# Experts' weights in rows of 48 KB: eight groups of six units a pair in three large places, the last norm's tables in the first norm's place

## The chip, the cores and the metric

One core of a Trainium2 chip runs the whole layer in one launch. The metric is the device time of that launch in microseconds, as the median of several runs; less is better. All numbers below come from the runs of the kernel before the change and from one profiled execution of it.

## What is computed

One post-norm layer of a bidirectional encoder over 512 tokens of width 1024, all in float32: a layer norm, a mixer (gated short convolution beside windowed attention), a second layer norm, a mixture of experts, a third layer norm. The change touches the experts and the third norm.

```python
def expert_choice_moe(x, w_router, w_gate, w_up, w_down):
    cap = CAPACITY_FACTOR * S // N_EXPERTS                      # 64 tokens an expert
    aff = jax.nn.softmax(jnp.einsum('bsd,de->bse', x, w_router), axis=-1)
    top_val, top_idx = lax.top_k(jnp.swapaxes(aff, 1, 2), cap)  # each of 16 experts picks its tokens
    xe = x[b_idx, top_idx]
    h = jax.nn.silu(jnp.einsum('becd,edf->becf', xe, w_gate)) * jnp.einsum('becd,edf->becf', xe, w_up)
    ye = jnp.einsum('becf,efd->becd', h, w_down) * top_val[..., None]
    return jnp.zeros_like(x).at[b_idx, top_idx].add(ye)
...
  f  = expert_choice_moe(x, ...)
  x  = layer_norm(ALPHA * x + f, ln2_g, ln2_b)
```

Each of the 16 experts has three matrices of 1024 x 2048 floats, so the experts' weights alone are 384 MB (of 1024 x 1024 bytes), and each of them is used once.

## The kernel before

The experts run as eight pairs (p = 0 to 7). The weights of a pair are cut into 48 **units** of 1 MB, 128 partitions by 2048 floats; unit m of pair p is number n = 48p + m, 0 to 383. Units 0 to 31 of a pair hold gate and up weights (line L999: eight matmuls a unit, `pg` or `pu`), units 32 to 47 hold the down weights (L1051, `d`). Between them PE has smaller work: gathering the tokens of the next pair (`g`, L904), transposing the hidden activations (`ht`, L1021) and the weights of the tokens (`oht`, L918), and adding the results back into the tokens' rows (`sc`, L1064). These small pieces stand in a list, `pend`, from which the loop takes one or two after each unit.

All weights come on SP's DMA queue, in the order in which they are used. SP does nothing else in this part; it waits until the place of a load is free (PE has finished with what lay there) and issues. Eight DMA semaphores are used in turn, so a DMA also waits for the one issued eight before it. The first units, 0 to `SMALL` - 1 = 79, come one at a time (`load_unit`, L591) into places of 8 KB a partition: 20 of them, R0 to R19, two of which later hold the sum `acc`, the place E (pool `extra`) and, once each, two working places. The list `places` (L882 and L883) gives the order. From unit 80 on, the memory of the small places R2 to R19 is used anew: four large places G0 to G3 of 32 KB a partition lie over R2 to R17, and behind them, in a pool `late`, the tables of the last norm (`c6`, `n6`, `rows6`, `left6`, `diag`, 9.5 KB a partition). A large DMA (L614) brings a **group** of four units, 32 KB a partition in one contiguous row; PE can start on a group when all of it has landed, and its place is free again when PE has used all four. In the last pair the groups from the fifth on (unit 16 of the pair on) are still four-unit places, but each unit is a DMA of its own (L617), the last one in three pieces (L621).

The last norm is written as a product: `last_rows` (L936) builds `c6`, turns it into `rows6` with transposes (L954) as pieces of `pend` in the last pair, and fills `n6` with constants; after the last weights, `n6` gets the norm's factors, is transposed into `left6` (L1111, L1112), and `left6` times `rows6` gives the rows' shifts (L1119). `diag` is a diagonal matrix of factors for the last tokens (L1107). The place E holds unit loads at first and, from pair 3, the second norm's rows (`ln1`) for the skip connection.

Of the kernel before, what the change touches and what calls it, by code (L numbers as in the profile page):

```python
# [10 lines left out]
F32 = mybir.dt.float32  # L11
F32R = mybir.dt.float32r
# [6 lines left out]
P = 128  # L19
D = 1024  # L20
S = 512
NT = S // P
KT = D // P
# [4 lines left out]
NE = 16  # L28
NPAIR = NE // 2
# [10 lines left out]
def encoder_layer(ctx: ExitStack, tc: tile.TileContext, x, ln0r, ln0c, w_in, conv_w, sink, w_ao, w_co, w_out,  # L40
# [18 lines left out]
    def wkt(i, shape, name):  # L59
        return shaped(wk.tile([P, 2048], F32, tag=f"W{i % 3}", name=name), shape)  # L60
# [523 lines left out]

    UNITS, SMALL = 48, 80
    units, groups = {}, {}

    def load_unit(n, pool, tag):
        t = pool.tile([P, 2048], F32, tag=tag, name=f"w_{n}")
        p, m = n // UNITS, n % UNITS  # L590
        pin(nc.sync.dma_start(t, w_moe[p, m // 4][:, m % 4]))  # L591
        return t

    def fetch(p, m):

        n = UNITS * p + m
        if n < SMALL:
            if n not in units:
                units[n] = load_unit(n, *places.pop(0))
            return units.pop(n)  # L600
        if not big:
            small.close()
            big.extend(ctx.enter_context(tc.tile_pool(name=f"big{i}", bufs=1, reuse_waits="tile")) for i in range(4))
            rest = ctx.enter_context(tc.tile_pool(name="late", bufs=1, reuse_waits="tile"))
            for name, shape, dt in (("c6", [P, KT, NT, 32], F32R), ("n6", [P, NT, 32], F32R), ("rows6", [P, D], F32R),
                                    ("left6", [P, P], F32R), ("diag", [P, P], F32)):
                late[name] = rest.tile(shape, dt, name=name)
        g, j = m // 4, m % 4
        if j == 0:
            i = (n // 4) % 4  # L610
            t = big[i].tile([P, 4, 2048], F32, tag=f"G{i}", name=f"w_{p}_{g}")
            src = w_moe[p, g]
            if p < NPAIR - 1 or g < 4:
                pin(nc.sync.dma_start(t, src))  # L614
            for i in range(4 if p == NPAIR - 1 and g >= 4 else 0):
                if (g, i) != (UNITS // 4 - 1, 3):
                    pin(nc.sync.dma_start(t[:, i], src[:, i]))  # L617
                else:
                    ends, begin = shaped(t[:, i], [2, 4, 256]), shaped(src[:, i], [2, 4, 256])
                    for f, n in ((0, 2), (2, 1), (3, 1)):  # L620
                        pin(nc.sync.dma_start(ends[:, :, f:f + n, :], begin[:, :, f:f + n, :]))  # L621
            groups[p, g] = t
        return groups[p, g][:, j]
# [258 lines left out]
    places = slots[:7] + [(wk, "W2")] + slots[7:8] + [(wk, "W0")] + slots[8:]  # L882
    places += [(extra, "E")] + slots + [(extra, "E")] + slots[2:] + [(extra, "E")] + slots[2:18]  # L883
    big = []
# [51 lines left out]
    def last_rows():  # L936
# [3 lines left out]
        nc.gpsimd.memset(c6.bitcast(F32), 0.0)  # L940
        nc.gpsimd.memset(n6.bitcast(F32), 0.0)
        for i, src in ((0, cols[:, 4, :]), (4, cols[:, 5, :])):
# [3 lines left out]
        nc.vector.tensor_copy(c6[:, :, :, 2:4], c6[:, :, :, 0:2].bitcast(F32))  # L946
        nc.vector.tensor_copy(n6[:, :, 4:6], onesq[:, :2 * NT].rearrange("p (t a) -> p t a", t=NT))

        def go(h):
# [6 lines left out]
            return part  # L956
        return [go(h) for h in range(2)]

# [26 lines left out]
    for p in range(NPAIR):  # L985
# [4 lines left out]
        for cbs in ([0, 1, 2], [3]) if p == 0 else ([cb] for cb in range(NCB)):  # L990
# [13 lines left out]
            for cb in cbs:  # L1004
                pss = acs[cb]
                if last and cb == 1:
                    ln2 = wkt(2, [1, D], "ln2")
                    pend.extend(spread(ln2, 4, 2))
                    ln2 = ln2[:, 0, :]
                    pend.extend(last_rows())  # L1010
# [167 lines left out]
```

## Time and profile before

| | us |
|---|---|
| median of 3 runs (1437.25 to 1438.56) | 1438.51 |
| the profiled execution | 1436.98 |
| its span | 1435.3 |
| PE busy | 1364.9 (95%) |
| DVE, ACT, POOL busy | 415.4, 292.8, 7.1 |
| weight DMAs of 4 MB: 68, median from issue to landing | 29.7 |
| weight DMAs of 1 MB: 111, median from issue to landing | 14.7 |

PE is TensorE; its busy time is modelled from pipelined matmuls, so 95% doesn't mean that it runs at its peak. The time from issue to landing of a DMA includes what was queued ahead of it. The mixer runs to about 500 us, the experts from there to 1420, the last norm after that.

### The profile page before, as it was taken

The page shows a single profiled execution, that of the slowest core. Times are in us where ns is not written, and L with a number is a line of the kernel's source. Part 1 is how long each engine was busy: PE and PEld are TensorE (multiplying, and loading weights), DVE is VectorE, ACT ScalarE, POOL GpSimd, SP SyncE. Part 2 cuts the span into 40 slices and gives each one's busy share as a digit, 9 for nine tenths or more (in the row PEclk, how much of TensorE's full clock was granted, in tenths as well). Part 3 has the DMA queues.
Part 4 walks back from the last instruction along what each step waited for, and adds up shares of the span by engine and source line. Part 5 has one row for each costly group of instructions (what it writes and reads, how often), then busy time and mean ns, then how long its engine had stood idle before and what let it go on. Part 6 is the DMA issues. An engine that isn't in the chain of part 4 may idle for free.

```text
span 1435.3 us, 15566 instructions
## 1 busy us (share of the span) xinstructions
PE 1364.9 (95%) x6586; PEld 738.2 (51%) x6586; DVE 415.4 (29%) x917; ACT 292.8 (20%) x569; POOL 7.1 (0%) x24
## 2 busy tenths in 40 slices
PE   8999999999999999999999898999989889889997
PEld 6778778788888843433333332332323233233344
DVE  7667666534535341011110010321011011001114
ACT  6654444423324211100000000100000000000110
POOL 1000000000000000000000000000000000000000
PEclk9999999999999999999999999999999999999999
DMA  4211222323236879999999999999999999999995
GB/s 171 96 60 59 89 88 85 121 88 102 104 118 260 354 287 397 422 421 424 432 431 430 431 431 432 431 429 434 428 435 427 434 427 434 429 434 429 417 422 226
DMA packets 36165, 450.96 MB, mean 314 GB/s; under 512 B 4608, under 2 KB 5248, under 8 KB 8320
## 3 DMA queue, kind: packets, MB, share of 16 engines
q1 hardware_dynamic: 34800, 446.28, 74.9%
q10 hardware_dynamic: 1296, 3.69, 0.7%
q8 instruction: 52, 0.85, 0.2%
q14 instruction: 17, 0.14, 0.0%
HBM read 447.85 MB, written 2.10 MB: 313 GB/s over the span
## 4 chain that ended last, share of the span: by engine, by line
PE 73%; DMA 24%; DVE 2%; ACT 1%; issue 0%; DVEq 0%; ACTq 0%; SPq 0%
DMA w<-in_w_moe 23%; PE pu L999 12%; PE pg L999 12%; PE d L1051 7%; PE g L904 4%; PE p_x L183 3%; PE p_b L183 3%; PE p_c L183 3%; PE p_q L183 3%; PE p_ga L183 3%; PE p_co L183 3%; PE p_ao L183 3%; PE p_gc L183 3%; PE sc L1064 3%; PE o L524 1%; PE s L484 1%
## 5 line engine op out<-in xcount | busy, mean ns | idle before, releaser
L999 PE MATMUL pg<-w,px 128*64 128x512 f32 x1024 | 245.3, 600 | 34.3 <-DMA w<-in_w_moe 34.3
L1051 PE MATMUL d<-w,hT 128*64 128x512 f32 (+1 forms) x1152 | 232.0, 553 | 20.0 <-DMA w<-in_w_moe 20.0
L999 PE MATMUL pu<-w,px 128*64 128x512 f32 x1024 | 246.4, 602 | 0.0
L999 PEld LDWEIGHTS pg<-w,px 128*64 128x64 f32 x1024 | 72.1, 137 | 183.6 <-issue 143.2
L1051 PEld LDWEIGHTS d<-w,hT 128*64 128x64 f32 x1152 | 81.9, 137 | 159.6 <-issue 150.0
L999 PEld LDWEIGHTS pu<-w,px 128*64 128x64 f32 x1024 | 66.8, 137 | 132.8 <-issue 130.5
L1013 DVE TENSOR_TENSOR h<-h,pu 128x512 f32<-128x512 f32 x32 | 22.0, 688 | 305.9 <-PE pu L999 305.9
L1069 DVE TENSOR_TENSOR acc<-acc,sc 128x512 f32<-128x512 f32 (+1 forms) x60 | 38.0, 634 | 249.8 <-PE sc L1064 249.7
L1012 ACT ACTIVATE h<-pg 128x512 f32<-128x512 f32 x32 | 19.1, 597 | 312.2 <-PE pg L999 294.2
L904 PEld LDWEIGHTS g<-px,xn 128*128 128x128 f32 x512 | 59.3, 192 | 23.0 <-issue 21.9
L1064 PE MATMUL sc<-ye,px 128*128 128x512 f32 (+1 forms) x136 | 66.9, 598 | 0.0
L904 PE MATMUL g<-px,xn 128*128 128x128 f32 x512 | 64.6, 281 | 0.2 <-DVE px L896 0.2
L1056 ACT COPY ye<-d 128x512 f32<-128x512 f32 (+1 forms) x18 | 9.7, 538 | 267.2 <-PE d L1051 267.2
L1064 PEld LDWEIGHTS sc<-ye,px 128*128 128x128 f32 x136 | 22.2, 191 | 45.5 <-issue 44.4
L183 PE MATMUL p_x<-yh,ws_x 128*128 128x512 f32 x128 | 43.9, 398 | 0.0
L183 PE MATMUL p_b<-yh,ws_b 128*128 128x512 f32 x128 | 43.9, 398 | 0.0
L183 PE MATMUL p_c<-yh,ws_c 128*128 128x512 f32 x128 | 43.7, 397 | 0.0
L183 PE MATMUL p_q<-yh,ws_q 128*128 128x512 f32 x128 | 42.1, 395 | 0.0
L911 ACT ACTIVATE px<-g,cols 128x128 f32<-128x128 f32 x32 | 14.6, 457 | 131.9 <-PE g L904 131.9
L496 ACT ACTIVATE pr<-pr,neg 128x256 f32<-128x256 f32 (+1 forms) x64 | 35.2, 553 | 28.7 <-DVE neg L492 28.7
L183 PE MATMUL p_ga<-yh,ws_ga 128*128 128x512 f32 x128 | 40.6, 391 | 0.0
L909 DVE TENSOR_SCALAR px<-g,cols 128x128 f32<-128x128 f32 x32 | 13.1, 409 | 94.3 <-ACT px L911 61.4
(279 smaller groups left out, 1648.5 us busy)
## 6 DMA issues: line engine op xcount, KB each, us to landing
w<-in_w_moe SPq DMA_DIRECT2D x68, 4096.0 KB, 29.7
w<-in_w_moe SPq DMA_DIRECT2D x111, 1024.0 KB, 14.7
raw_q<-in_w_in SPq DMA_DIRECT2D x4, 1024.0 KB, 4.8
raw_c<-in_w_in SPq DMA_DIRECT2D x4, 1024.0 KB, 4.9
raw_x<-in_w_in SPq DMA_DIRECT2D x4, 1024.0 KB, 4.8
raw_b<-in_w_in SPq DMA_DIRECT2D x4, 1024.0 KB, 4.9
raw_ga<-in_w_in SPq DMA_DIRECT2D x4, 1024.0 KB, 4.8
raw_gc<-in_w_in SPq DMA_DIRECT2D x4, 1024.0 KB, 4.9
```

Source lines behind the costliest of these rows:

```text
L183: put(nc.tensor.matmul(ps, ws[:, a, k, :], (opnd.lo if b else opnd.hi)(k), start=(k + a + b == 0), stop=ends))
L484: nc.tensor.matmul(ps, q, k[:, g, keys], start=(i == 0), stop=(i == 1))
L496: nc.scalar.activation(p, p, AF.Exp, bias=self.neg[:, i:i + 1], accum_out=self.su[:, i:i + 1])
L524: nc.tensor.matmul(pa[half * 64:half * 64 + 64, :256], vt[g][:, self.b0 + j, :], self.pT[:, j, :, half, :], start=(j == 0), stop=(j == sel ...
L904: pin(nc.tensor.matmul(ps[:, i * P:(i + 1) * P], xt[t][:, (k + i) * P:(k + i + 1) * P], oh1[:, t].rearrange("p a c -> p (a c)"), start=(t ...
L911: nc.scalar.activation(xe[:, j, :], src, AF.Identity, bias=cols[:, 3, j:j + 1], scale=cols[:, 2, j:j + 1])
L999: pin(nc.tensor.matmul(acs[cb][i][hs, :], xe[:, kk, hs], wt[:, a, k, :], start=(kk == 0), stop=(kk == KT - 1)))
L1012: nc.scalar.activation(hb, pss[0], AF.Silu)
L1013: nc.vector.tensor_tensor(hb, hb, pss[1], OP.mult)
L1051: pin(nc.tensor.matmul(pd[hs, :width], hTs[p][:, f, hs], wt[:, a, ft, :], start=(f == 0), stop=(f == 15)))
L1064: pin(nc.tensor.matmul(ps[:, :width], ohT[:, t * P:(t + 1) * P], ye, start=True, stop=True))
L1069: nc.vector.tensor_tensor(a, a, ps[:, :width], OP.add)
```

## The change

The weights lie in memory as eight groups of six units a pair, so that a group is one row of 48 KB a partition, and there are three large places of 48 KB instead of four of 32 KB. They cover R2 to R19 completely, six small places each. `SMALL` is 78 instead of 80, so that the groups of six fall on the pairs' boundaries (78 = 48 + 30). In the last pair the units come one at a time from its fourth group on, which is unit 18 instead of 16. Since the large places leave no room for the pool `late`, the tables of the last norm go elsewhere: `c6` and `rows6` into the place E, `n6` and `left6` into the memory of `c6` when it has been transposed, `diag` behind `ln2` in a working place. The filling of `n6` therefore moves into a piece of its own, `factors`, behind the two pieces that read `c6`.

```diff
--- before.py
+++ after.py
@@ -582,13 +582,13 @@
 
 
 
-    UNITS, SMALL = 48, 80
+    UNITS, SMALL = 48, 78
     units, groups = {}, {}
 
     def load_unit(n, pool, tag):
         t = pool.tile([P, 2048], F32, tag=tag, name=f"w_{n}")
         p, m = n // UNITS, n % UNITS
-        pin(nc.sync.dma_start(t, w_moe[p, m // 4][:, m % 4]))
+        pin(nc.sync.dma_start(t, w_moe[p, m // 6][:, m % 6]))
         return t
 
     def fetch(p, m):
@@ -600,20 +600,16 @@
             return units.pop(n)
         if not big:
             small.close()
-            big.extend(ctx.enter_context(tc.tile_pool(name=f"big{i}", bufs=1, reuse_waits="tile")) for i in range(4))
-            rest = ctx.enter_context(tc.tile_pool(name="late", bufs=1, reuse_waits="tile"))
-            for name, shape, dt in (("c6", [P, KT, NT, 32], F32R), ("n6", [P, NT, 32], F32R), ("rows6", [P, D], F32R),
-                                    ("left6", [P, P], F32R), ("diag", [P, P], F32)):
-                late[name] = rest.tile(shape, dt, name=name)
-        g, j = m // 4, m % 4
+            big.extend(ctx.enter_context(tc.tile_pool(name=f"big{i}", bufs=1, reuse_waits="tile")) for i in range(3))
+        g, j = m // 6, m % 6
         if j == 0:
-            i = (n // 4) % 4
-            t = big[i].tile([P, 4, 2048], F32, tag=f"G{i}", name=f"w_{p}_{g}")
+            i = ((n - SMALL) // 6) % 3
+            t = big[i].tile([P, 6, 2048], F32, tag=f"G{i}", name=f"w_{p}_{g}")
             src = w_moe[p, g]
-            if p < NPAIR - 1 or g < 4:
+            if p < NPAIR - 1 or g < 3:
                 pin(nc.sync.dma_start(t, src))
-            for i in range(4 if p == NPAIR - 1 and g >= 4 else 0):
-                if (g, i) != (UNITS // 4 - 1, 3):
+            for i in range(6 if p == NPAIR - 1 and g >= 3 else 0):
+                if (g, i) != (UNITS // 6 - 1, 5):
                     pin(nc.sync.dma_start(t[:, i], src[:, i]))
                 else:
                     ends, begin = shaped(t[:, i], [2, 4, 256]), shaped(src[:, i], [2, 4, 256])
@@ -880,7 +876,7 @@
     for i in range(2, 20):
         slots.append((small.enter_context(tc.tile_pool(name=f"r{i}", bufs=1, reuse_waits="tile")), f"R{i}"))
     places = slots[:7] + [(wk, "W2")] + slots[7:8] + [(wk, "W0")] + slots[8:]
-    places += [(extra, "E")] + slots + [(extra, "E")] + slots[2:] + [(extra, "E")] + slots[2:18]
+    places += [(extra, "E")] + slots + [(extra, "E")] + slots[2:] + [(extra, "E")] + slots[2:16]
     big = []
     order0 = [8 * cb + 2 * kq + i for kq in range(4) for cb in range(3) for i in range(2)]
     for n in order0[1:23]:
@@ -938,13 +934,16 @@
 
         c6, n6, rows6 = late["c6"], late["n6"], late["rows6"]
         nc.gpsimd.memset(c6.bitcast(F32), 0.0)
-        nc.gpsimd.memset(n6.bitcast(F32), 0.0)
         for i, src in ((0, cols[:, 4, :]), (4, cols[:, 5, :])):
             wide = src[:, :, None].to_broadcast([P, KT, NT])
             nc.vector.tensor_copy(c6[:, :, :, i], wide)
             nc.vector.tensor_tensor(c6[:, :, :, i + 1], wide, c6[:, :, :, i].bitcast(F32), OP.subtract)
         nc.vector.tensor_copy(c6[:, :, :, 2:4], c6[:, :, :, 0:2].bitcast(F32))
-        nc.vector.tensor_copy(n6[:, :, 4:6], onesq[:, :2 * NT].rearrange("p (t a) -> p t a", t=NT))
+
+        def factors():
+
+            nc.gpsimd.memset(n6.bitcast(F32), 0.0)
+            nc.vector.tensor_copy(n6[:, :, 4:6], onesq[:, :2 * NT].rearrange("p (t a) -> p t a", t=NT))
 
         def go(h):
             def part():
@@ -954,7 +953,7 @@
                     pin(nc.tensor.transpose(ps[:, k * P:(k + 1) * P], src, ident))
                 nc.scalar.copy(rows6[:, 512 * h:512 * h + 512], ps)
             return part
-        return [go(h) for h in range(2)]
+        return [go(h) for h in range(2)] + [factors]
 
     acc = None
     ln2 = None
@@ -1004,7 +1003,14 @@
             for cb in cbs:
                 pss = acs[cb]
                 if last and cb == 1:
-                    ln2 = wkt(2, [1, D], "ln2")
+                    home = wk.tile([P, 2048], F32, tag="W2", name="ln2")
+                    ln2 = shaped(home, [1, D])
+                    both6 = extra.tile([P, 2048], F32R, tag="E", name="rows6")
+                    late["c6"] = both6[:, :D].rearrange("p (k t c) -> p k t c", k=KT, t=NT)
+                    late["rows6"] = both6[:, D:]
+                    late["n6"] = both6[:, :P].rearrange("p (t c) -> p t c", t=NT)
+                    late["left6"] = both6[:, P:2 * P]
+                    late["diag"] = home[:, D:D + P]
                     pend.extend(spread(ln2, 4, 2))
                     ln2 = ln2[:, 0, :]
                     pend.extend(last_rows())
@@ -1149,6 +1155,8 @@
     w_in = chunks(a["w_in"][0], 256)
     halves = w_in[CHUNK_K].reshape(P, KT, 2, P).transpose(0, 2, 1, 3)
     w_in = np.concatenate([w_in[:CHUNK_K], halves.reshape(1, P, KT, 256), w_in[CHUNK_K + 1:]])
+    w_moe = np.concatenate([both, np.concatenate([down(a["w_down"][0][:NE - 2], 2), down(a["w_down"][0][NE - 2:], 4)])], axis=1)
+    w_moe = w_moe.transpose(0, 1, 3, 2, 4).reshape(NPAIR, 8, 6, P, 2048).transpose(0, 1, 3, 2, 4)
     lay = {
         "x": a["x"][0],
         "ln0r": np.stack([a["ln0_g"], a["ln0_b"]]),
@@ -1161,7 +1169,7 @@
         "w_out": a["w_out"][0].reshape(2, 4, P, 2, 512).transpose(3, 0, 2, 1, 4),
         "ln1c": per_partition(a["ln1_g"][0], a["ln1_b"][0]),
         "w_router": a["w_router"][0].reshape(KT, P, NE).transpose(1, 0, 2),
-        "w_moe": np.concatenate([both, np.concatenate([down(a["w_down"][0][:NE - 2], 2), down(a["w_down"][0][NE - 2:], 4)])], axis=1),
+        "w_moe": w_moe,
         "ln2c": per_partition(a["ln2_g"][0], a["ln2_b"][0]),
     }
     nc = bacc.Bacc("TRN2", target_bir_lowering=False, num_devices=1, dynamic_dma_scratch_size=1024)
```

Where it shows, first: SP, at the change from units to groups. The names are the loads of single units (2048 floats a partition) and of groups (w_8 is group 8 of pair 1). Before:

```order
L591 DMA w_4922<-in_w_moe 128x2048 [waits DMAHW6_49,PE_49]
L591 DMA w_4928<-in_w_moe 128x2048 [waits DMAHW7_49,PE_49]
L591 DMA w_4934<-in_w_moe 128x2048 [waits DMAHW0_49,PE_49]
L591 DMA w_4940<-in_w_moe 128x2048 [waits DMAHW1_49,PE_49]
L614 DMA w_8_5021<-in_w_moe 128x8192 [waits DMAHW2_49,PE_49]
L614 DMA w_9_5039<-in_w_moe 128x8192 [waits DMAHW3_49,PE_49]
L614 DMA w_10_5060<-in_w_moe 128x8192 [waits DMAHW5_49,DMAHW4_49,PE_49]
```

SP at the same place, after (w_5 is the sixth group of pair 1, units 78 to 83):

```order
L591 DMA w_4922<-in_w_moe 128x2048 [waits DMAHW6_49,PE_49]
L591 DMA w_4928<-in_w_moe 128x2048 [waits DMAHW7_49,PE_49]
L610 DMA w_5_4961<-in_w_moe 128x12288 [waits DMAHW0_49,PE_49]
L610 DMA w_6_5024<-in_w_moe 128x12288 [waits DMAHW3_49,DMAHW4_49,DMAHW2_49,DMAHW5_49,DMAHW1_49,PE_49]
L610 DMA w_7_5065<-in_w_moe 128x12288 [waits DMAHW7_49,DMAHW6_49,PE_49]
```

The two single loads of units 78 and 79 are gone, and the first group stands directly behind unit 77; its wait for PE is for the six units (64 to 69) that lay in its place, where it was four (64 to 67).

Second: PE, at the fourth and fifth unit of the last pair (w_0 and w_1 are that pair's first two groups, px the gathered tokens, oht a transpose). Before:

```order
L999 MATMUL pu_0_6903<-w_0_6904,px_6779 64x512 x4
L999 MATMUL pg_0_6902<-w_1_6944,px_6779 64x512 [waits DMAHW3_49,Activation_49]
L999 MATMUL pg_0_6902<-w_1_6944,px_6779 64x512
L999 MATMUL pg_0_6902<-w_1_6944,px_6779 64x512 [waits DVE_49]
L999 MATMUL pg_0_6902<-w_1_6944,px_6779 64x512
```

PE at the same place, after:

```order
L998 MATMUL pu_0_6846<-w_0_6847,px_6726 64x512 x4
L998 MATMUL pg_0_6845<-w_0_6847,px_6726 64x512 [waits Activation_49]
L998 MATMUL pg_0_6845<-w_0_6847,px_6726 64x512
L998 MATMUL pg_0_6845<-w_0_6847,px_6726 64x512 [waits DVE_49]
L998 MATMUL pg_0_6845<-w_0_6847,px_6726 64x512
L914 MATMUL oht_6892<-ident,px_6726 128x128 [waits DVE_49]
L914 MATMUL oht_6892<-ident,px_6726 128x128 x3
L998 MATMUL pu_0_6846<-w_0_6847,px_6726 64x512 x4
L998 MATMUL pg_0_6845<-w_1_6902,px_6726 64x512 [waits DMAHW4_49,Activation_49]
```

The matmuls stand in the same order; the wait for the second group has moved from the fifth unit of the pair to the seventh.

## Rows read from the trace of the kernel before

**Rows 1.** The page: GB/s in 40 slices of 35.9 us; the chain by line.

```profile
GB/s 171 96 60 59 89 88 85 121 88 102 104 118 260 354 287 397 422 421 424 432 431 430 431 431 432 431 429 434 428 435 427 434 427 434 429 434 429 417 422 226
...
DMA w<-in_w_moe 23%; PE pu L999 12%; PE pg L999 12%; PE d L1051 7%; PE g L904 4%; PE p_x L183 3%; PE p_b L183 3%; PE p_c L183 3%; PE p_q L183 3%; PE p_ga L183 3%; PE p_co L183 3%; PE p_ao L183 3%; PE p_gc L183 3%; PE sc L1064 3%; PE o L524 1%; PE s L484 1%
```

**Rows 2.** Windows: length; busy PE, PEld, DVE, ACT, POOL; granted clock; DMA share; GB/s.

```profile
560.00:650.00 90.00, 90.00 (x431) 34.42 (x428) 10.72 (x20) 9.47 (x17) 0.00 (x0) 1.00 1.01 422
...
780.00:1300.00 520.00, 469.53 (x2155) 173.46 (x2157) 64.45 (x115) 38.56 (x70) 0.00 (x0) 0.99 1.00 431
1340.00:1370.00 30.00, 30.00 (x140) 10.20 (x138) 2.07 (x3) 4.62 (x8) 0.00 (x0) 1.00 1.01 421
```

**Rows 3.** The chain in order of time: start, duration; a DMA from issue to landing.

```profile
808.37 31.43 DMA w<-in_w_moe
...
928.53 27.85 DMA w<-in_w_moe
...
1277.71 31.41 DMA w<-in_w_moe
...
1370.63 19.81 DMA w<-in_w_moe
...
1390.50 19.80 DMA w<-in_w_moe
```

**Rows 4.** DMA issues from 808.3-928.5, 1370.6-1390.5, and at 498.4, 649.7, 669.0: median to landing.

```profile
w<-in_w_moe SPq DMA_DIRECT2D x12, 4096.0 KB, 30.6
...
w<-in_w_moe SPq DMA_DIRECT2D x8, 1024.0 KB, 19.8
...
w<-in_w_moe SPq DMA_DIRECT2D x1, 1024.0 KB, 4.7
...
w<-in_w_moe SPq DMA_DIRECT2D x1, 1024.0 KB, 18.5
...
w<-in_w_moe SPq DMA_DIRECT2D x1, 4096.0 KB, 13.8
```

**Rows 5.** Timeline of PE, units 67, 69 and 78: start, duration.

```profile
667.11 1.89 PE L999 MATMUL pu<-w,px 128*64 128x512 f32 x8
...
670.54 1.89 PE L999 MATMUL pu<-w,px 128*64 128x512 f32 x8
...
686.73 1.89 PE L999 MATMUL pg<-w,px 128*64 128x512 f32 x8
```

**Rows 6.** Waits (total, times, longest): SP from 655 to 672, PE from 668 to 1310.

```profile
SPq L614 <- PE pu L999: 13.2, 1, 13.2
...
PE d L1051 <- DMA w<-in_w_moe: 18.4, 9, 3.9
```

**Rows 7.** Timeline of PE: pair 6's last six units; pair 7's units 0, 6, 12, 35.

```profile
1297.80 10.52 PE L1051 MATMUL d<-w,hT 128*64 128x512 f32 x48
...
1309.26 1.94 PE L999 MATMUL pg<-w,px 128*64 128x512 f32 x8 [0.94 <-DMA w<-in_w_moe]
...
1324.61 1.89 PE L999 MATMUL pg<-w,px 128*64 128x512 f32 x8
...
1338.53 1.89 PE L999 MATMUL pg<-w,px 128*64 128x512 f32 x8
...
1388.10 1.95 PE L1051 MATMUL d<-w,hT 128*64 128x256 f32 x16 [0.37 <-DMA w<-in_w_moe]
```

**Rows 8.** Waits from 1300 to the end: total, times, longest.

```profile
PE d L1051 <- DMA w<-in_w_moe: 1.7, 4, 0.5
```

**Rows 9.** Windows behind two of eight long waits, columns as in rows 2.

```profile
820.50:823.90 3.40, 3.39 (x12) 1.23 (x12) 0.35 (x1) 0.00 (x0) 0.00 (x0) 1.00 1.03 443
...
1289.60:1292.90 3.30, 3.30 (x8) 0.90 (x5) 0.00 (x0) 0.00 (x0) 0.00 (x0) 0.50 1.07 459
```

**Rows 10.** The tile n6: count, ns min/median/max, first and last start.

```profile
L941 POOL MEMSET n<- x1: 204/204/204, 658.2 to 658.2; 128x128 f32 x1
L947 DVE CAST n<-onesq x1: 167/167/167, 658.5 to 658.5; 128x8 fp32r<-128x8 f32 x1
```

## Prediction

> **What bounds the kernel now.** I read the 40 slices first [rows 1]: from the seventeenth (574 us on) nearly to the end the DMA engines move 417 to 435 GB/s, while before that they have room. The chain of waits [rows 1] has 23% of the span in the experts' weights, so I then took the stretches apart by windows [rows 2]. From 560 to 650 us PE has no idle time and the DMA engines are full as well, because PE uses up a lead that was built earlier. From 780 to 1300 us PE idles 50 of 520 us, nearly all of it for weights, and the stream runs at 431 GB/s. So two things set the end: a stream of weights that must not pause after 560 us, since nothing later makes a pause good, and what PE still has to do when the stream ends. I call 1 MB of weights a unit, and number the units 0 to 383 (48p+m).
>
> **The pace of the stream.** The chain names landings: a group of 4 units issued at 808.37 lands 31.43 later, at 839.80, and one issued at 928.53 lands at 956.38, with 12 groups issued from the first up to the second [rows 3, 4]; that is 116.58/12 = 9.715 us per 4 MB. Single units: 1370.63+19.81 and 1390.50+19.80, eight units apart, 19.86/8 = 2.483 us per MB [rows 3, 4]. A straight line through the two (rows of 8 and of 32 KB) gives 2.411 us per MB and 0.072 us per DMA, so a 6 MB group takes an estimated 14.54 us.
>
> **A. The hand-over from small to large DMAs: +6.5 us.** Before, units 78 and 79 are small, and the first large group waits until units 64 to 67 are used up. PE ends unit 67 at 667.11+1.89 = 669.00 [rows 5], and the group, issued at 669.0, lands 13.8 later [rows 4]. On an empty queue 1 MB lands 4.7 us after its issue [rows 4], 2.2 more than its 2.48, so 4 MB would land after 11.9: something was still in the queue, and the stream did not pause. But SP had stood 13.2 us for PE there [rows 6], so little was left in it. After, the last small unit is 77, which lands at 649.7+18.5 = 668.2 [rows 4], and the first group of six covers the places of units 64 to 69, so it waits for unit 69, which PE ends at 670.54+1.89 = 672.43 [rows 5]. By then the queue has been empty for 4.3 us, and the 2.2 us of an empty queue come on top. So the group lands at 672.47+2.2+14.54 = 689.2, against 668.2+14.54 = 682.7 without a pause: 6.5 us lost. Behind this waiting DMA stand all later groups on SP. The second group waits for unit 75, which PE has used up before it reaches unit 78 at 686.73 [rows 5], while the first is still in transfer: the pause happens once. PE waits at unit 78 for some 2.5 us, which costs nothing beyond the pause, since PE waits for the stream later anyway.
>
> **B. Longer rows: -1.8 us.** The change carries 276 units (78 to 353) in 46 groups: 46 x 14.537 = 668.7 us. Before, 272 of them went in 68 groups and 4 as single units: 68 x 9.715 + 4 x 2.483 = 670.5 us. Bounds: at the rate of the 4 MB groups 6 MB take 14.57 and the gain is 0.2; with no fixed part left at all (2.411 per MB) 14.465, and the gain is 5.1. I take the line's value, since two sizes lie on it. A+B: the stream ends 4.7 us later.
>
> **C. The last pair: +2.4 us more.** PE starts pair 7 when its first group has landed (1277.71+31.41 = 1309.12 [rows 3], start 1309.26 [rows 7]). That group now has six units instead of four. What is left of the stream after it is shorter by two single units (4.97) and by 3 x 9.715 - 2 x 14.537 = 0.07: PE starts 5.0 us nearer to the stream's end. Then PE is the bound: it waits 0.94 us before the first unit, then for no weights up to 1388.10 [rows 7], and 1.7 us in four waits from there [rows 8]. A unit that follows at once starts 0.17 before the modelled end of the one before it and lasts 1.89 instead of 1.95, so four waits give back 1.7 + 4 x 0.23 = 2.6. 5.0 - 2.6 = 2.4 us of PE's work are left over when the stream ends. I looked whether PE would still wait for groups two and three of the pair: it comes to its seventh unit 15.3 us after its start (1324.61) and to its thirteenth 29.3 after (1338.53) [rows 7], against 14.5 and 29.1 for the landings; it does not, by a hair. The last unit's pieces and the last norm stay as they are.
>
> **D. The clock at the start of pair 7: +0.8 us.** Before that start PE has only the last six units of pair 6, 10.5 us of pure matmul (1297.80) [rows 7], against 14.54 for the transfer: a wait of 4.0 us, where it was 0.94. Of eight waits of 2 us or more in this trace, four were followed by a stretch of 3.3 us at a granted clock of 0.50 (1.2 of 2.4 GHz), as at 1289.6, and four by none, as at 820.5 [rows 9]. Half of 3.3 us is lost: 1.65. Everywhere else in the stream's stage the next wait swallows that; here all of PE's later work is on the path. Bounds 0 and 1.65; the eight waits split evenly, so I take the middle. (The longest, 3.9 [rows 6], is the one before 820.5, with no drop.)
>
> **E. The tables of the last norm: 0.** The same transposes and copies run, one piece later in pair 7. The zeroing of the second small table (0.20 us on POOL) and its copy (0.17 on DVE) [rows 10] move behind the transposes that read the memory they share, where DVE is busy 2.07 of 30 us and POOL not at all [rows 2]. They are needed only in the last norm. Without that cover they would cost their 0.4 us. The zeroing of the large table now waits for the skip that reads the first norm's rows in the same place, which pair 3 and 4 run.
>
> **Sum.** 6.5 - 1.8 + 2.4 + 0.8 = +7.9 us. The profiled execution took 1436.98 (span 1435.3), so it would take 1444.9; the median of the runs shown is 1.5 higher, 1438.51, and becomes 1446.4, which I forecast. With the bounds: 6.5 - 5.1 + 2.4 = 3.8 (1442.3) to 6.5 - 0.2 + 2.4 + 1.65 = 10.4 (1448.9).
>
> **The rivals.**
> 1. Faster: the longer row pays as much again. From 8 to 32 KB a MB went from 2.483 to 2.429, 2.2% less. The same step once more gives 14.25 per group, 46 x 14.25 = 655.5, B = -15.0, and 1433.2. It decides from 14.37 per group on. Against it: the line needs only a fixed part per row, of which 0.072 of 9.715 is left. 2%.
> 2. Faster: each DMA pays a fixed time in line. There are 182 weight DMAs now and 156 after; at the 2.2 us that an empty queue shows, 26 fewer save 57 us: near 1390. Against it: a group takes 9.715 us and four single units 9.93, so three DMAs fewer save 0.22 us, not 6.6. 1%. The Trainium skill, DMA: Bandwidth & Descriptors, section "Anatomy of one DMA", gives such a law for DMAs from GpSimd, about 2.0 us fixed plus bytes over 436 GB/s. By it, 26 fewer would save an estimated 52 us. The trace agrees with its fixed part only on an empty queue (4.7 us for 1 MB), which is the case of A, not of the full queue of B.
> 3. Within 0.2%: the pause of A doesn't come, because something keeps the queue filled or the group waits for fewer places. That leaves 1.4 us: 1439.9. Against it: its six places are those of units 64 to 69, and SP stood 13.2 us there already. 4%.
> 4. PE catches up in pair 7, with C and D gone: 1443.2. For it: 2.4 us in 109 is little. 8%.
> 5. The 48 KB rows go as 32 and 16: one more fixed part per group, 14.61 us, B = +1.6, 1449.8. No row shows a size between. 5%.
> 6. Three places are too few. A group must be used up 2 x 14.54 - 2.2 = 26.9 us after it lands, else the stream pauses again. PE is busy 470 of 520 us [rows 2], 13.1 us per 14.54, so it decides only if PE runs at half clock nearly throughout. A pause of 2 us in each of five pairs would make 1456. 3%.
>
> **Chances.** The forecast with its bounds 77%. A measurement can tell about 0.2%, 2.9 us, from no change. Faster by more: rivals 1 and 2, 3%. Within: rival 3 and the lowest corner, 5%. Slower: 92%. The range 1442.3 to 1449.2 holds the forecast's bounds and rival 4, 85%, which leaves some of it for the spread of the runs (1437.25 to 1438.56).
>
> **What would show it.** Right: the first large group is issued near 672.5 and lands near 689, with a dip in GB/s around 670; groups then land every 14.5 us; PE waits about 4 us before pair 7 and then hardly at all for weights, and its last weights matmul ends some 7 us later. Wrong: no dip, or a 6 MB cadence under 14.4 or over 14.6; waits for weights late in pair 7 (then C falls); an end that moves away from PE's last unit in the last norm (then E falls).

## The result

| | us |
|---|---|
| after, median of 5 runs (1445.83 to 1448.64) | 1447.35 |
| before beside it, median of 5 runs (1437.02 to 1438.56) | 1437.97 |
| ratio, with its 95% interval | 1.0067 [1.0056, 1.0078] |
| the profiled execution of after; its span | 1445.83; 1444.0 |

The change costs 9.4 us. The forecast was +7.9 and 1446.4. (The ratios here and below are estimated from all runs; they are not the quotient of the two medians.) The profiled execution of after was the fastest of the five; three more profiles of it follow below.

The page of after, GB/s in 40 slices of 36.1 us and the chain by line (beside [rows 1]):

```profile
GB/s 170 96 59 59 88 88 88 117 89 115 88 117 268 344 310 404 421 421 321 435 433 435 434 429 433 430 431 433 433 434 433 431 435 430 428 433 433 416 421 211
...
DMA w<-in_w_moe 21%; PE pu L998 12%; PE pg L998 12%; PE d L1057 8%; PE g L900 5%; PE p_x L183 3%; PE p_b L183 3%; PE p_c L183 3%; PE p_q L183 3%; PE p_ga L183 3%; PE sc L1070 3%; PE p_gc L183 3%; PE p_co L183 2%; PE p_ao L183 2%; PE o L524 1%; PE s L484 1%
```

The nineteenth slice (650 to 686 us) fell from 424 to 321 GB/s; from the sixteenth to the thirty-ninth all others stand within 2% of before. That is the hand-over. DMA issues of after at 650.8 (unit 77) and at 673.6 (the first group), and SP's waits from 655 to 680 (beside [rows 4, 6]):

```profile
w<-in_w_moe SPq DMA_DIRECT2D x1, 1024.0 KB, 17.4
...
w<-in_w_moe SPq DMA_DIRECT2D x1, 6144.0 KB, 19.0
...
SPq L610 <- PE pu L998: 22.4, 1, 22.4
```

Unit 77 lands at 668.24 and the group, issued at 673.59, at 692.55: 24.31 us between two landings where 14.53 is the pace, a pause of 9.8. The pace itself stands in the chain of after, two landings three groups apart, and the issues between them (beside [rows 3]):

```profile
1012.70 30.15 DMA w<-in_w_moe
1057.81 28.63 DMA w<-in_w_moe
...
w<-in_w_moe SPq DMA_DIRECT2D x3, 6144.0 KB, 30.6
```

(1086.44 - 1042.85)/3 = 14.53 us per 6 MB; the median over all 45 gaps is 14.534. PE of after at unit 78, the first of the large places, at the last units of pair 6, at the start of pair 7, and at its last weights (start, duration, wait before; beside [rows 5, 7]), then PE's waits for weights from 1310 to 1440 (beside [rows 8]):

```profile
692.60 2.83 PE L998 MATMUL pg<-w,px 128*64 128x512 f32 x6 [4.57 <-DMA w<-in_w_moe]
...
1307.71 10.52 PE L1057 MATMUL d<-w,hT 128*64 128x512 f32 x48
1320.60 1.94 PE L998 MATMUL pg<-w,px 128*64 128x512 f32 x8 [2.37 <-DMA w<-in_w_moe]
...
1424.94 3.67 PE L1057 MATMUL d<-w,hT 128*64 128x256 f32 x32
...
PE pg L998 <- DMA w<-in_w_moe: 2.4, 1, 2.4
```

In this execution PE waits 2.37 us for pair 7's first group and then for no weights at all; its last matmul on weights ends at 1428.62. Before, it ended at 1419.99. The last norm behind it takes 15.42 us now and 15.27 before.

### The profile page after: what moved, and what is told of

Read it like the earlier page. It is cut to its first block, busy times and chain, and to the rows that moved or that the text cites. A ratio compares the mean times of both kernels' runs of the same rounds, so it can differ in the third digit from the quotient of the medians.

```text
span 1444.0 us, 15489 instructions
## 1 busy us (share of the span) xinstructions
PE 1373.9 (95%) x6586; PEld 741.3 (51%) x6586; DVE 415.6 (29%) x917; ACT 292.8 (20%) x569; POOL 7.4 (1%) x24
## 4 chain that ended last, share of the span: by engine, by line
PE 73%; DMA 22%; DVE 3%; ACT 1%; issue 1%; SPq 0%; DVEq 0%; ACTq 0%
DMA w<-in_w_moe 21%; PE pu L998 12%; PE pg L998 12%; PE d L1057 8%; PE g L900 5%; PE p_x L183 3%; PE p_b L183 3%; PE p_c L183 3%; PE p_q L183 3%; PE p_ga L183 3%; PE sc L1070 3%; PE p_gc L183 3%; PE p_co L183 2%; PE p_ao L183 2%; PE o L524 1%; PE s L484 1%
## 5 line engine op out<-in xcount | busy, mean ns | idle before, releaser
L998 PE MATMUL pg<-w,px 128*64 128x512 f32 x1024 | 256.0, 622 | 51.7 <-DMA w<-in_w_moe 51.7
L1057 PE MATMUL d<-w,hT 128*64 128x512 f32 (+1 forms) x1152 | 226.9, 547 | 0.9 <-DMA w<-in_w_moe 0.9
L907 ACT ACTIVATE px<-g,cols 128x128 f32<-128x128 f32 x32 | 14.6, 457 | 151.8 <-PE g L900 151.8
```

Of the source, the lines that this page charges most:

```text
L907: nc.scalar.activation(xe[:, j, :], src, AF.Identity, bias=cols[:, 3, j:j + 1], scale=cols[:, 2, j:j + 1])
L998: pin(nc.tensor.matmul(acs[cb][i][hs, :], xe[:, kk, hs], wt[:, a, k, :], start=(kk == 0), stop=(kk == KT - 1)))
L1057: pin(nc.tensor.matmul(pd[hs, :width], hTs[p][:, f, hs], wt[:, a, ft, :], start=(f == 0), stop=(f == 15)))
```

## The experiments

Each ran beside the kernel before on the same chip. That kernel took 1437.97 us beside after, 1437.93 beside the first four experiments, 1437.31 beside the next four and 1437.73 beside the last version; where kernels of different groups are compared below, each is taken by its distance from the kernel before beside it. What the runs ask is: is the loss the pause, does the row's length pay as the line says, and what do the last pair and the tables cost.

**The hand-over alone, in the kernel before.** Four single units fewer, nothing else:

```diff
-    UNITS, SMALL = 48, 80
+    UNITS, SMALL = 48, 76
...
-            i = (n // 4) % 4
+            i = ((n - SMALL) // 4) % 4
...
-    places += ... + [(extra, "E")] + slots[2:18]
+    places += ... + [(extra, "E")] + slots[2:14]
```

> The kernel before with four single units fewer ahead of the large places (76 instead of 80) and nothing else: 32 KB rows, four places, the tables where they were. The first large DMA still waits until unit 67 is used up, but the last single unit is now 75, whose DMA lands near 663.2 us, so the queue runs empty before PE ends unit 67 (669.0 in the profile of before). My theory (the stream pauses at the hand-over, and nothing gives a pause back): the first group lands at 669.04 + 2.2 + 9.7 = 681.0 instead of 663.2 + 9.7 = 672.9, a pause of 8.0 us, and the kernel is about 7.8 us slower than before (1445.8). Rival (a pause is made good, because PE waits for weights later and what it has to do is the same; the loss of the changed kernel lies in its larger groups): the pause stands in the trace, but the time is that of before within 2 us.

Measured: 1447.27 us against 1437.93, ratio 1.0068 [1.0055, 1.0081]. The same dip stands in its page:

```profile
GB/s 166 99 59 59 88 87 88 117 91 113 88 120 267 339 317 399 422 421 311 431 428 433 433 433 428 431 432 430 432 432 432 430 430 432 432 430 429 418 422 219
```

The first group was issued at 670.84 and landed 13.4 us later, 19.21 after the last single unit: a pause of 9.5 us where 8.0 was expected. With 32 KB rows, four places and the old tables a pause of this size costs 9.3 us, as much as the whole change. So it is not made good later, and the rival has fallen.

**The changed kernel without the pause.** 102 single units, so that the first group waits for a unit that lies 14 units back instead of 9:

```diff
-    UNITS, SMALL = 48, 78
+    UNITS, SMALL = 48, 102
...
-    places += ... + slots[2:] + [(extra, "E")] + slots[2:16]
+    places += ... + slots[2:] + [(extra, "E")] + slots[2:]
+    places += [(extra, "E")] + slots[2:] + [(extra, "E")]
```

> The changed kernel with 102 instead of 78 single units, so that the first large DMA waits for a unit that stands 14 units ahead of it instead of 9: no pause at the hand-over; rows of 48 KB, three places and the moved tables stay. My theory: the 9.8 us of pause that the trace of the changed kernel shows between units 77 and 83 go, and 24 single units instead of four groups cost 24 x 2.483 - 4 x 14.53 = 1.5 us: about 8.3 us faster than the changed kernel, 1439 us, 1 us slower than before. Rival one (the pause costs nothing in the end): within 2 us of the changed kernel, 1447. Rival two (three places are too few, and the stream pauses elsewhere when it is no longer late): the dip goes, other gaps over 14.6 us between landings come in pairs 3 to 6, and the time is in between.

Measured: 1439.73 us, ratio 1.0013 [1.0005, 1.0022]: 7.6 us under the changed kernel, where 8.3 was expected. The dip is gone, and no new one came:

```profile
GB/s 162 99 65 59 88 88 84 122 88 105 101 117 243 363 288 402 421 421 420 422 438 433 428 433 436 428 432 434 431 433 432 433 429 431 432 433 434 413 421 184
```

Its groups land 14.53 us apart (the median), as in after. The second rival's sign, gaps over 14.6 us, does show in three places: landings at 832.69, 1066.74 and 1329.84 come 16.1 us after the one before. But these three DMAs had been issued 31 to 32 us ahead, so the queue wasn't empty; such late landings stand in before too, and are taken up below. So three places of 48 KB are enough. In its profiled execution (1441.26 us) PE waits 4.08 us before pair 7, a half-clock stretch of 6.83 us begins in that wait, and the last matmul on weights ends 5.1 us after the stream: what the last pair costs is still in this kernel.

**The tables alone.** The kernel before, with `c6`, `rows6`, `n6`, `left6` and `diag` where the change puts them:

```diff
-            rest = ctx.enter_context(tc.tile_pool(name="late", bufs=1, reuse_waits="tile"))
...
+                    both6 = extra.tile([P, 2048], F32R, tag="E", name="rows6")
```

> The kernel before with the tables of the last norm moved alone, and its weights loaded as they were. My theory: no change, within 0.2% of before (1438), because the tables are built far ahead of their use and the tail of the kernel is the same. Rival: the tables' new place delays the last norm or the first transfers into the place that they took, and 1 to 3 us of the changed kernel's 9 are from here.

Measured: 1437.89 us against 1437.93, ratio 1.0003 [0.9994, 1.0012]. The tables cost nothing. In after the late zeroing stands on POOL at 1369, some 60 us before its use:

```profile
1369.36 0.20 POOL L945 MEMSET rows<- 128x128 f32 x1 [415.14 <-PE rows L953]
```

**Is the slow restart due to the 48 KB rows?** The first group alone as six DMAs of 1 MB:

```diff
-            if p < NPAIR - 1 or g < 3:
+            single = n == SMALL or (p == NPAIR - 1 and g >= 3)
+            if not single:
                 pin(nc.sync.dma_start(t, src))
-            for i in range(6 if p == NPAIR - 1 and g >= 3 else 0):
+            for i in range(6 if single else 0):
...
```

> The changed kernel, with the first large group alone loaded as six DMAs of 1 MB into its place, issued in a row when the place is free. In the trace of the changed kernel this group, issued at 673.59 into an empty queue, lands 18.96 us later, that is 4.4 us more than a group's 14.53; a 1 MB DMA on an empty queue lands 2.2 us after its 2.48. My theory (a DMA with 48 KB rows starts more slowly on an empty queue than one with 8 KB rows): the sixth unit lands 2.2 + 6 x 2.48 = 17.1 us after the first issue, 1.9 us earlier, the PE wait of 4.6 us at unit 78 goes, and so does the half-clock stretch behind it; the time is 1.9 us under the changed kernel's, 1445.5. Rival (the 4.4 us are the price of any restart at that moment, not of the long rows): landing and time stay as in the changed kernel, within 0.5 us.

Measured: 1447.42 us, no gain; the time that I expected didn't come. Its DMA issues at 672.5 (the first unit of the six) and at 683.5 (the group behind them):

```profile
w<-in_w_moe SPq DMA_DIRECT2D x1, 1024.0 KB, 5.0
...
w<-in_w_moe SPq DMA_DIRECT2D x1, 6144.0 KB, 21.9
```

The first unit lands 5.0 us after its issue, 2.5 over its 2.48, and the sixth at 689.86, 17.37 us after the first issue: near the 17.1 expected, 2.5 us over the pace, and earlier than the first group of after (18.96, or 4.4 over). But the group behind lands 15.59 us after it, at 705.45, instead of 14.53, and so the two together take 32.96 us, 3.5 over the pace of 29.43. In after the same two groups took 33.48, 4.4 over. With 32 KB rows (the first experiment, two groups) the sum was 3.7 over the pace, with 24 KB rows (below, four DMAs) 4.5.

The 15.59 isn't the restart's. In every trace here a landing that is late by up to 1.6 us comes back, some 215 to 265 us later, with the queue full; here are four traces, each with the landings of one such row and by how much they came late:

| kernel | landing (late by) |
|---|---|
| this one | 705.45 (1.05), 954.05 (1.01), 1202.64 (1.00), 1419.07 (0.97) |
| after, second execution (below) | 706.14 (0.94), 954.56 (0.76), 1203.13 (0.76), 1417.06 (0.77) |
| the tables alone | 682.84 (0.75), 917.48 (0.76), 1152.28 (0.96), 1393.02 (0.95) |
| the last version (below) | 683.93 (0.25), 917.98 (0.24), 1166.55 (0.25), 1394.84 (0.22) |

So of the rival the time stands and the landing doesn't: the pause over the two groups, 8.8 us, lies among those of after (8.2 to 9.8). Whether long rows start more slowly isn't settled: six single units lost 2.5 us by themselves, while the first group of 48 KB rows lost between 3.1 and 4.4 in the four executions of after, and how much of that was such a late landing can't be told.

**The last number that sets the pause.** The last 14 single units go four places further on, so that the first group waits for unit 65 instead of 69:

```diff
-    places += [(extra, "E")] + slots + [(extra, "E")] + slots[2:] + [(extra, "E")] + slots[2:16]
+    places += [(extra, "E")] + slots + [(extra, "E")] + slots[2:] + [(extra, "E")] + slots[6:]
```

> The changed kernel with one number changed: the last 14 single units go into the single places 6 to 19 instead of 2 to 15, so that the first large place (single places 2 to 7) waits for unit 65 instead of unit 69. Rows of 48 KB, three places, 78 single units and the moved tables stay. My theory (the whole change is the hand-over's pause, less what the longer rows give, plus what the last pair costs): the first group is issued some 7 us earlier, near 666.5, about 1.7 us before unit 77 has landed, and the pause of 9.8 us shrinks to 1 to 3 us; the kernel takes 7 to 9 us less than the changed one, 1439.5. The gain of the longer rows (1.9) is then at last in the stream's end, but the last pair's 0.8 and a half-clock stretch at its start (0 to 2.3) take it back: same as before within 0.2%. Rival (with 48 KB rows and three places the stream pauses elsewhere): over 1442.

Measured: 1440.88 us (1438.32 to 1442.01), ratio 1.0019 [1.001, 1.0028]; 3.6 us over the kernel before, and so 5.8 under the changed kernel, where 7 to 9 were expected. The pause is gone altogether: the group is issued at 665.81 and lands 14.53 us after unit 77. But a new loss shows ahead of it. DMA issues of units 64 to 69, first in after, then in this kernel:

```profile
w<-in_w_moe SPq DMA_DIRECT2D x6, 1024.0 KB, 16.1
```

```profile
w<-in_w_moe SPq DMA_DIRECT2D x6, 1024.0 KB, 7.6
```

They land 7.6 us after their issue instead of 16.1, since each waits for a place that PE leaves four units later. So little lies in the queue by then that four of the landings, of units 64, 65, 66 and 69, come 2.60, 3.08, 4.13 and 2.98 us after the one before instead of 2.49: 2.8 us lost (some 0.5 of it may be a late landing of the kind above, which shows in this trace at 889.3 and 1137.9).

**The last pair in single units.** In the changed kernel, pause and all:

```diff
-            if p < NPAIR - 1 or g < 3:
+            if p < NPAIR - 1:
                 pin(nc.sync.dma_start(t, src))
-            for i in range(6 if p == NPAIR - 1 and g >= 3 else 0):
+            for i in range(6 if p == NPAIR - 1 else 0):
```

> The changed kernel with all 48 units of the last pair in single DMAs; the hand-over and its pause stay. The stream gets 18 x 2.483 - 3 x 14.53 = 1.1 us longer. My theory (at the start of the last pair PE waits for a whole group of six, falls back to half clock in part of the runs, and ends 2.9 to 5.1 us after the stream instead of 2.05): PE no longer waits 2 to 4 us for the pair's first unit, there is no half-clock stretch at its start, and the last matmul on weights ends 2.05 us after the stream's end; 1.1 - 0.8 - 1.5 = about 1.2 us under the changed kernel's median, 1446.2, with a smaller spread. Rival (the granularity of the last pair costs nothing): 1.1 us over the changed kernel, 1448.5.

Measured: 1445.44 us (1444.87 to 1446.23), ratio 1.0055 [1.0041, 1.0069]: 8.1 us over the kernel before, and so 1.3 under the changed kernel with a longer stream, as expected, and a spread of 1.4 us instead of 2.8. PE no longer stands before pair 7 (44 of the 48 matmuls on the last six units of pair 6, then the first unit of pair 7, without a wait), and its last matmul on weights ends 2.04 us after the stream:

```profile
1307.44 9.61 PE L1057 MATMUL d<-w,hT 128*64 128x512 f32 x44
1316.89 1.89 PE L998 MATMUL pg<-w,px 128*64 128x512 f32 x8
```

**Both at once.** Shifted places (the edit shown above), and the last pair's three groups in halves of 24 KB rows:

```diff
...
-            if p < NPAIR - 1 or g < 3:
-                pin(nc.sync.dma_start(t, src))
+            cut = 3 if p == NPAIR - 1 else 6
+            for i in range(0, 6 if p < NPAIR - 1 or g < 3 else 0, cut):
+                pin(nc.sync.dma_start(t[:, i:i + cut], src[:, i:i + cut]))
```

> The kernel of the shifted places with, in the last pair alone, each of the three large groups in two DMAs of three units (24 KB rows). By the line of the prediction two DMAs of 3 MB take 14.61 us against 14.53, so the stream gets 0.24 us longer. My theory: PE starts the pair on the first half, without the wait of 2 to 4 us and the half clock behind it, and ends 2.05 us after the stream: about 2 us under the kernel of the shifted places alone, 1437.5, as fast as before or up to 1 us faster, since the 1.9 us of the longer rows now stay. Rival (the spread of the changed kernel has another cause than the wait at the last pair): the time of the shifted places alone, within 0.5 us.

Measured: 1437.94 us against 1437.31, ratio 1.0003 [0.9994, 1.0012], 2.9 us under the shifted places alone. PE at the end of pair 6 (again 44 of the 48 matmuls) and the start of pair 7:

```profile
1299.44 9.61 PE L1058 MATMUL d<-w,hT 128*64 128x512 f32 x44
1308.88 1.89 PE L999 MATMUL pg<-w,px 128*64 128x512 f32 x8
```

No wait stands between the two. With the shifted places alone PE waited 4.09 us there, in the profiled execution, and a half-clock stretch of 3.41 us began at the end of that wait. So the rival has fallen.

**Every group in halves.** Two DMAs of 3 MB (24 KB rows) instead of one of 6 MB, all else as in after:

```diff
-                pin(nc.sync.dma_start(t, src))
+                for h in range(2):
+                    pin(nc.sync.dma_start(t[:, 3 * h:3 * h + 3], src[:, 3 * h:3 * h + 3]))
```

> The changed kernel with every group of six as two DMAs of three units each (24 KB rows), the places, waits and order left as they are. The line that the prediction used for longer rows (2.411 us per MB and 0.072 us per DMA) gives 14.61 us per group instead of 14.53, 46 x 0.07 = 3.4 us over the whole stream, and PE can start on the first half of a group 7 us earlier, so its waits of 4 us and the half clock behind them go: 3.4 - 2.3 = 1.1 us over the changed kernel, 1448.5. Rival one (a fixed time per DMA of 2.0 us that shows in the stream): 14.53 + 2 per group, 1540. Rival two (the length of the row doesn't matter between 24 and 48 KB, the gain of the changed kernel's cadence is from the larger group): 14.53 per group, and 1445.

Measured: 1447.67 us, ratio 1.0068 [1.0055, 1.0081]: 10.4 us over the kernel before, and so 1.0 over after, as expected (1.1). Its chain, two landings, and the issues from the first of these DMAs up to the second:

```profile
1006.98 30.32 DMA w<-in_w_moe
1052.27 28.85 DMA w<-in_w_moe
...
w<-in_w_moe SPq DMA_DIRECT2D x6, 3072.0 KB, 33.7
```

(1081.12 - 1037.30)/6 = 7.303 us per 3 MB; the median of 89 gaps is 7.302. The line of the prediction gives 3 x 2.411 + 0.072 = 7.305. Rival one falls by the cadence, and rival two too (7.27 per 3 MB by it). From unit 77's landing to the stream's end, less the pause, it takes 3.7 us longer than the first profile of after (3.4 expected); PE gives most of that back, because it starts pair 7 on a half group and ends 2.06 us after the stream.

**A version that takes the best of each.** As the kernel with both, but units 64 and 65 keep the early places 2 and 3:

```diff
-    places += ... + [(extra, "E")] + slots[6:]
+    places += ... + [(extra, "E")] + slots[2:4] + slots[8:]
```

> As the kernel with shifted places and halves in the last pair, but the last 14 single units go into the single places 2, 3 and 8 to 19 (instead of 6 to 19). The first large place still waits for unit 65 alone. In the traces of the two kernels with places 6 to 19 the landings of units 64 to 69 fell behind their 2.49 us pace by 2.6 to 3 us in all, since each of them waited for a place that came free four units later than before. My theory (that loss, and not a price of the large groups, is why the kernel with halves was no faster than before): units 64 and 65 keep their early places, only units from 66 on wait longer, by when the queue is deeper, and the loss falls to about 1 us: 1.5 to 2 us under the kernel with halves, 1436.2, about 0.1% faster than before. Rival (the loss at units 64 to 69 is given back anyway): 1437.9, as the kernel with halves.

Measured: 1437.41 us against 1437.73, ratio 0.9999 [0.999, 1.0008]. No change from before can be told. By the kernel before beside each it is 1.0 us under the kernel with both, not 1.5 to 2. The landings from unit 67 to 69 still fell back by 1.2 us; with 0.24 for the halves that takes most of the 1.9 that the longer rows give. (The first group's 0.25 stands in the table above: it comes back in mid stream.) No kernel here beats the one before.

**Why the changed kernel's times differ by 3 us.** Three more executions of it, unchanged:

> The changed kernel once more, for the profile of a second execution. My theory (the executions of the changed kernel differ by up to 3 us because PE, after its wait for the first group of the last pair, falls to half clock in some of them): if the time is near 1447.4 or above, its trace has a half-clock stretch of 2 to 7 us in the last pair and its last matmul on weights ends 4 to 5 us after the stream, against 2.85 in the first profile (1445.83 us, no stretch there); if the time is near 1446, neither. Rival (the difference comes from when the stream of weights starts): the last matmul ends 2.9 us after the stream's end whatever the time, and the stream's end moves.

> The changed kernel a third time. Both profiles so far (1445.83 and 1445.09 us) lie at the low end of its times and show no half clock in the last pair. My theory: an execution near 1447.4 or above has a half-clock stretch of 2 to 7 us inside the last pair, and its last matmul on weights ends 4 to 5 us after the stream. Rival (the slower executions start or feed the stream later): it ends about 3 us after the stream at any time, and the stream's end is near 1427 or 1428.

> The changed kernel a fourth time, with the same question and the same expectations as the third.

Measured, beside the first profile and before:

| execution | time | pause | stream ends | wait before pair 7 | half clock in pair 7 | last weights matmul after the stream |
|---|---|---|---|---|---|---|
| before | 1436.98 | none | 1417.93 | 0.94 | 0 | 2.06 |
| after, first | 1445.83 | 9.8 | 1425.77 | 2.37 | 0 | 2.85 |
| after, second | 1445.09 | 9.0 | 1424.70 | 2.83 | 0 | 3.24 |
| after, third | 1448.40 | 9.6 | 1424.97 | 4.11 | 5.94 | 6.19 |
| after, fourth | 1446.82 | 8.2 | 1424.06 | 4.10 | 3.42 | 5.51 |

PE of the third at the start of pair 7, and two windows there (columns as in [rows 2]; the third number from the end is the granted clock):

```profile
1320.43 1.97 PE L998 MATMUL pg<-w,px 128*64 128x512 f32 x4 [4.11 <-DMA w<-in_w_moe]
...
1319.60:1326.30 6.70, 5.87 (x18) 3.11 (x19) 0.00 (x0) 0.00 (x0) 0.00 (x0) 0.50 0.96 413
1326.40:1333.10 6.70, 6.70 (x41) 3.72 (x42) 0.71 (x2) 0.76 (x2) 0.00 (x0) 1.00 1.03 441
```

At 0.50 (1.2 of 2.4 GHz) PE ran 18 matmuls in the 5.87 us that it was busy; at 1.00 it ran 41 in 6.70. The third execution's stream ends 0.8 us before that of the first, and it takes 2.6 us longer. From PE's start in pair 7 to its last weights matmul it took 110.73 us, against 107.88 and 108.02 in the two without such a stretch. The rival falls. My expectation stands as to the cause, with two misses: the last matmul came 6.2 and 5.5 us after the stream, not 4 to 5, and the fourth execution had a stretch at 1446.82 us, under the 1447.4 that I had named.

## Why the prediction was right, step by step

**The likeliest case came, and its sum was near: +7.9 forecast, +9.4 measured.** By the mean of the four profiles of after the terms are A +9.1, B -1.9, C +1.3 and D +1.1, together +9.6, as much as these four took over the profiled execution of before. That the sum came within 1.5 us of the measured +9.4 is luck in part: A was 2.6 too small and C 1.1 too large.

**A, the pause: the mechanism was right, the size too small (6.5; measured 8.2 to 9.8).** The first group waited for unit 69 and came into an empty queue, once. Two things were mis-sized. The first group landed 17.6 to 19.0 us after its issue, 3.1 to 4.4 over the pace, where I took the 2.2 of a lone 1 MB DMA [rows 4]. The recurring late landings have a share in that which can't be told apart everywhere: in the second execution one fell on the second group (15.47) and is counted in the pause of 9.0; in the first, late landings at 926.56 (1.15) and 1175.12 (1.12) make it likely, though not shown, that the one before them fell near 678, when the first group was under way. And PE was at unit 69 up to 1.1 us later than in the one execution of before that I read: the first group was issued between 672.47 and 673.59. What I had read off one execution to 0.1 us moves by a microsecond between executions.

**B, the longer rows: -1.8 forecast, -1.9 measured.** From unit 77's landing to the stream's end it is 757.53 us in the first profile of after and 749.73 before; less the pause of 9.78 that leaves -2.0 (the others give -2.1, -2.0 and -1.6). The pace, 14.534 us per 6 MB, is the line's 14.537, and the halves put a fourth size on the line. The rivals of a row that pays twice, of a fixed time per DMA in the full queue, and of 48 KB rows cut in two (14.61) fall with that.

**C, the last pair: +2.4 forecast, some +1.3 measured.** PE's part was right: its pair 7 got 2.7 and 2.9 us shorter in the two executions without half clock (2.6 forecast), and no wait for weights is left. The stream's part was not 5.0 but 3.5 to 4.7: from PE's start in pair 7 to the stream's end it took 105.17, 104.64, 104.54 and 103.99 us, against 108.67 before. The recurring late landings move this: in the first profile of after one fell on a single unit in pair 7 (3.59 us after the one before instead of 2.48), and in the profile of before one (1.24) fell on pair 7's own first group. The 0.94 us that PE waited there, which the prediction took as a fixed part, came from it: in the kernel with the tables alone, whose stream is the same, PE starts pair 7 without a wait, 109.42 us before the stream's end.

**D, the clock before pair 7: +0.8 forecast, 0, 0, 2.8 and 1.5 measured.** The mechanism was right, the upper bound of 1.65 was too low. I had seen stretches of 3.4 us; in after they are also 6.83 us long. In the four executions the wait before pair 7 was under 3 us in the two without a stretch, and 4.1 in the two with one. This is most of the spread of the changed kernel's times.

**E, the tables: nothing, as forecast.** The end did not move away from PE's last weights.

What stays open: what a restart costs by itself (2.5 us with the six single units, at most 4.4 in after) and whether the row's length has a share in it, what makes landings late some 215 to 265 us apart, and when a wait is followed by half clock. In the first profile of after nine waits of 3.2 to 4.6 us between 688 and 1280 were each followed by a stretch, and two of 2.7 and 2.9 were not; but before, the longest of all, 3.9 us, was followed by none [rows 6, 9], and one of 2.1 us at 1003 was.

## What to carry to other kernels

Where a stream of weights sets the end, a larger transfer unit is paid for at its seams: count for the first large place which small units must be used up, when the last small one lands, and keep its issue ahead of that landing; 3.0 us was enough here. (Issued 4.0 us ahead it landed without a pause, in the kernel with shifted places. Issued 3.5 us ahead, in the last version, and 3.0 us ahead, in the kernel with the tables alone, it landed 0.25 and 0.75 late, but both come back in mid stream by the table above, so they are no price of the hand-over. No run issued it later than that and still ahead of the landing.) Then count what the consumer has left to do when the last large piece has landed, and cut the last pieces small. The gain of the larger DMA with its longer row was 1.9 us of 670; the seam took five times as much.

## What the runs showed of the hardware

- The time of a weight DMA in a full queue lies on one line through four sizes: 1 MB 2.485, 3 MB 7.302, 4 MB 9.713, 6 MB 14.534 us (medians; rows of 8, 24, 32 and 48 KB), that is 2.411 us per MB and 0.07 us per DMA. The row and the DMA grow together here, so no run tells a cost per row from a cost per DMA.
- A restart on an empty queue: a lone 1 MB DMA landed 2.2 to 2.5 us later than its share of the pace, six of 1 MB in a row 2.5, the first 4 MB 3.7, and the first 6 MB 3.1 to 4.4 (four executions of after). By the Trainium skill, DMA: Bandwidth & Descriptors, section "Anatomy of one DMA", a DMA issued from GpSimd has a fixed part of about 2.0 us, mostly for the completion. The lone 1 MB DMA on this other queue agrees with it; the restart of the stream measured up to twice as much.
- Late landings in a full queue come back in each trace: before has 1.26, 1.23 and 1.24 us at 820.38, 1064.75 and 1309.12, the first profile of after 1.15, 1.12 and 1.11 at 926.56, 1175.12 and 1403.21. What sets them off isn't shown.
- From 650 us to pair 7, PE ran 14 us at half clock in the profile of before and 38 to 44 in those of after, and nothing of it shows in the end there, where the stream sets the pace; 3.4 and 5.9 us of it in pair 7 cost 1.5 and 2.8 us.
